# A two-layer diffusion trunk on one core: the first down projection turns finished rows into columns from the next group's fourth step on, and the first feed-forward's block sums are issued in three calls per channel group

## The chip, the core and the metric

The kernel runs on one core of a Trainium2 chip. The metric is the device time of one execution in microseconds (us); a few executions are timed and their median is given. Beside the timed runs one execution is profiled; every duration below comes from that one. The engines are TensorE (PE; its weight loads are listed as PEld), VectorE (DVE), ScalarE (ACT), GpSimd (POOL) and SyncE (SP), which only issues transfers. Each engine works through its own list of instructions in order, and waits at an instruction until what it needs is there. PEclk is the TensorE clock that was granted, as a share of full speed.

## The reference

Two layers over 1024 latent tokens and 256 context tokens, width 1024. Cut to what matters here:

```python
for l in range(2):
    h = rmsnorm(x, norm_mix_pre[l]) * (1 + sc1) + sh1      # latent and context apart
    m = hybrid_mixer(h, ...)      # attention heads and a conv + state-space scan, one in- and one out-projection
    x = x + g1 * rmsnorm(m, norm_mix_post[l])
    f = rmsnorm(x, norm_ffn_pre[l]) * (1 + sc2) + sh2
    y = (silu(f @ w_gate[l]) * (f @ w_up[l])) @ w_down[l]  # 1024 -> 2816 -> 1024
    x = x + g2 * rmsnorm(y, norm_ffn_post[l])
return x_lat                                               # context is not updated in the last layer
```

All of it is float32.

## The kernel before

**Products.** Each float32 product is made of three: weights and activations are split into a high part (a cast, on ACT, L114 for weights) and a low part (the difference, on POOL or DVE, L115), and `mm3` issues high*high, high*low and low*high on L228, L229 and L230. A weight tile is thus loaded raw (`raw_t`, `raw_u`; L126, issued by SP), cast by ACT, and subtracted by POOL; only then can PE use it (`w_t`, a ring of five).

**Rows and columns.** The residual stream x is kept as ten tiles of 128 tokens: tiles 0 and 1 are context, 2 to 9 latent. A projection needs it the other way round, with channels on the partitions. That takes a rescale of the rows by 1/rms (`pre_scale`: squares on ACT L243, the small sums and the root on POOL L245, L235 and L236, and the multiplication of the rows in place on POOL L375) and then a "flip": transposes on PE (L402 in `flip_steps`, two tiles and two channel blocks in one PSUM bank), two ACT evictions that apply scale and shift (L405), a high part on POOL (L409) and a low part on DVE (L410). The results are `hc` (context), `ha` and `hb` (the two halves of the latent tokens).

**The first feed-forward.** In layer 0, `ctx_gateup` multiplies the context by the gate and up weights, 22 steps of 128 hidden channels with 48 products of 256 columns each (0.118 us apiece). After each step it calls `next(fill)` once. The fill, `fill_c`, prepares the latent tokens for the gate and up projections that come next. These use seven block products in the place of eight, and so need sums and differences of 2x2 blocks: `quads` loads two flipped blocks (L1009), transposes two more (L1016, evicted by ACT on L1020), keeps one of them in DRAM (L1032, L1033), forms four differences on DVE and puts each with its high (ACT, L1025) and low part (L1026) into the blocks `T1` to `T4`. It does that for two pairs of tiles (i) and two channel groups (k2) each, and comes back to its caller once per channel group. In layer 1 the same `quads` is run to its end in one go.

**The down projection and its end.** `down_all` works in groups of tiles: in layer 0 tiles 0 to 3, then 4 to 6, then 7 to 9 (groups 0, 1 and 2 below). A group runs over 22 steps `ff`; a step multiplies one weight tile of 128x1024 with the hidden values of each tile of the group (`hid_ring`, loaded on L1201 by SP, eight slots in all), 6 products of 512 columns per tile. A tile's sums stay in two PSUM banks for the whole group; there are five banks of the kind `ps_w` and three of the kind `ps_s`. At the last step of a group `finish_psum` ends each tile: squares on ACT from the banks, the root on POOL, a multiplication on DVE (L832) that frees the banks, the addition to x (L838, on POOL for even tiles, on DVE for odd ones), and a store of the new x to DRAM, issued by ACT (L839). Then `done` hands the tile on: with every second tile it rescales the pair at once (`pre_scale`, in place, so it has to wait until the store has read the rows), and puts the pair's flip into the list `todo`. `flip` takes one step (four transposes and what follows) from that list after each step `ff` of groups 1 and 2:

```python
                    def done(t, y):
                        ys[t] = y
                        if t in pairs:
                            xs = [ys[t - 1], y]
                            k.pre_scale(xs)
                            todo.append(k.flip_steps(xs, *pairs[t], 1, 0))
```

What is left in the list (the last two pairs, which make `hb`) is flipped in layer 1, inside `xbc`, which starts layer 1's in-projection with a few products on `hc` and `ha`, goes on with those on `hb`, and copies each result into a row buffer on ACT (L483). Its conv weights are loaded on L463 and L464 and transposed on L466.

**What sets the order.** The code names the work in the order above, but a scheduler with its own estimates of durations and priorities decides in which order each engine's list is written. Moving a call in the code moves the instructions of every engine near it, and not always by as much as the code says.

Of the kernel before, what the change touches and what calls it, by code (L numbers as in the profile page):

```python
# [54 lines left out]
class Trunk:  # L55
# [945 lines left out]
    def quads(self, l, xs, i, B):  # L1001
        nc = self.nc
        cc = self.cols[l, 1]
        tt = nc.vector.tensor_tensor
        v = lambda a: a.rearrange("p (k n) -> p k n", k=2)
        for k2 in range(0, 4, 2):
            qa, qb = self.x(), self.x()
            for half in range(2):
                nc.sync.dma_start(qa[:, half * 512:(half + 1) * 512], self.hf_d[l][(k2 + 4 * half) // 2, i])  # L1009
            for half in range(2):  # L1010
                t = self.psw()
                for k in range(2):
                    kt = k2 + 4 * half + k
                    for j, a in enumerate(xs):
                        rows = a[half][:, kt % 4 * P:(kt % 4 + 1) * P] if isinstance(a, list) else a[:, kt * P:(kt + 1) * P]
                        nc.tensor.transpose(t[:, k * 256 + j * P:k * 256 + (j + 1) * P], rows, self.ident)  # L1016
                for k in range(2):
                    kt = k2 + 4 * half + k
                    o = half * 512 + k * 256
                    nc.scalar.activation(qb[:, o:o + 256], t[:, k * 256:(k + 1) * 256], AF.Identity, bias=cc[:, kt:kt + 1], scale=cc[:, 16 + kt:17 + kt])  # L1020
            b11, b21, b12, b22 = qa[:, 0:512], qa[:, 512:1024], qb[:, 0:512], qb[:, 512:1024]

            def put(name, src, eng):
                d = B[name][:, k2:k2 + 2, :, 256 * i:256 * i + 256]
                nc.scalar.copy(d[:, :, 0], v(src))  # L1025
                eng.tensor_tensor(d[:, :, 1], v(src), d[:, :, 0].bitcast(F32), op=ALU.subtract)  # L1026

            if l:
                put("B22", b22, nc.vector)
            else:  # L1030
                keep = self.s2()
                nc.gpsimd.tensor_scalar(keep, b22, 1.0, 1.0, op0=ALU.mult, op1=ALU.mult)  # L1032
                nc.scalar.dma_start(self.b22_d[k2 // 2, i], keep)  # L1033
            tt(b11, b12, b11, op=ALU.subtract)
            tt(b12, b22, b12, op=ALU.subtract)
            tt(b22, b22, b11, op=ALU.subtract)
            put("T2", b22, nc.vector)
            put("T3", b12, nc.vector)
            put("T1", b11, nc.vector)
            tt(b21, b22, b21, op=ALU.subtract)  # L1040
            put("T4", b21, nc.gpsimd)
            yield
# [163 lines left out]
    def down_all(self, l, hx, load, fill=lambda: None, done=lambda t, x: None):  # L1206
        loads = self.loads
        ahead = 9 if l else 8
        for n in range(3, ahead):
            load(n)  # L1210
        for n, (g, ff) in enumerate(loads):
            ts = self.GROUPS[l][g]
            if ff == 0:
                banks = [[a(), b()] for a, b in ((self.psw, self.psw), (self.psw, self.psw), (self.pss, self.pss), (self.psw, self.pss))[:len(ts)]]
            h, u = hx.pop(n), self.U[l, "d", g, ff]
            for i, t in enumerate(ts):
                for c in range(2):
                    s = slice(c * 512, (c + 1) * 512)
                    self.mm3(banks[i][c], (h[:, 0, i * P:(i + 1) * P], h[:, 1, i * P:(i + 1) * P]), (u[:, 0, 0, s], u[:, 1, 0, s]),
                             ff == 0, ff == NFF - 1)  # L1220
                if ff == NFF - 1:
                    done(t, self.finish_psum(l, t, banks[i]))
            self.free(l, "d", g, ff)
            load(n + ahead)
            if g:
                fill()

    def finish_psum(self, l, t, halves):
# [7 lines left out]
def emit(nc, tc, I, out, dump=None):  # L1236
    with ExitStack() as es:
        k = Trunk(nc, tc, es, I, out)
# [13 lines left out]
        def drain(*gs):  # L1252
            for g in gs:
                for _ in g:
                    pass

        for l in range(DEPTH):
# [62 lines left out]
            with tc.tile_pool(name=f"acc{l}", bufs=1, reuse_waits="tile") as accp:  # L1320
                if l == 0:
                    B = {}

                    def fill_c():
                        fl[2]()
                        yield
                        xs = [k.row_halves(t, 0) for t in (6, 7)]
                        B.update(k.blocks(accp))
                        yield
                        for i in range(2):  # L1330
                            k.pre_scale(xs)
                            yield
                            for _ in k.quads(0, xs, i, B):
                                yield
                            if i == 0:
                                xs = [k.row_halves(t, 0) for t in (8, 9)]
                                yield

                    k.spare = (lambda: accp.tile([P, 1024], F32, tag="raw", name="raw_u"),
                               lambda: k.grp.tile([P, 1024], F32, tag="grow", name="raw_u"))  # L1340
                    fc = fill_c()
                    k.ctx_gateup(0, fc)
                    drain(fc)
                    k.back22(B)

                    def fill_s():
                        yield from k.mod_stream(0, (5,), k.psw, True)
                        yield from k.mod_stream(1, (0, 1), k.psw, True)
                        cols = k.mod_cols(1, 0)
                        yield from k.mod_stream(1, (2,), k.psw, True)  # L1350
                        cols()
                        yield from k.mod_stream(1, (3, 4, 5), k.psw, True)

                    fs = fill_s()
                    hx, load = k.ffn(0, B, step(fs), accp)
                    drain(fs)
                    k.frow = [k.gate_row(0, 5, "norm_ffn_post", 0), k.gate_row(0, 5, "norm_ffn_post", 1, k.x())]
                    ys, todo = {}, []
                    pairs = {1: (SC, 0), 3: (SA, 0), 5: (SA, 1), 7: (SB, 0), 9: (SB, 1)}

                    def done(t, y):
                        ys[t] = y
                        if t in pairs:
                            xs = [ys[t - 1], y]
                            k.pre_scale(xs)
                            todo.append(k.flip_steps(xs, *pairs[t], 1, 0))

                    def flip():
                        while todo and next(todo[0], todo) is todo:
                            todo.pop(0)  # L1370

                    k.down_all(0, hx, load, flip, done)
                    late = [lambda: drain(todo.pop(0))] * len(todo)
                else:
                    B = k.blocks(accp)
                    B["B22"] = k.block22()
                    k.down_all(1, *k.ffn(1, B, lambda: None, accp, fl[2], [k.last_x[t] for t in (8, 9)]))
# [23 lines left out]
```

## Time and profile before

| | |
|---|---|
| median of 3 runs | 3217.45 us (3215.97 to 3223.33) |
| profiled execution, its own time | 3221.04 us |
| its span in the trace | 3219.3 us |
| mean granted TensorE clock | 0.973 |
| busy: PE, PEld | 94%, 78% |
| busy: DVE, ACT, POOL | 52%, 44%, 52% |

The profiled execution's own time is 1.7 us longer than its span and 3.6 us longer than the median. A row of the wait view reads: engine, the tile written and its line, "<-", the releaser with its tile and line, then the summed wait in us, the number of waits and the longest. A row of the timeline reads: start in us from the span's start, duration, engine, line, operation, out<-in, shapes, how many instructions were put together, and in brackets how long the engine had waited and for what. A row of the table by stretch reads: the stretch, its length, then the busy time (and number of instructions) of PE, PEld, DVE, ACT and POOL, the granted clock, the share of the DMA engines and GB/s.

### The profile page before, as it was taken

The page shows a single profiled execution, that of the slowest core. Times are in us where ns is not written, and L with a number is a line of the kernel's source. Part 1 is how long each engine was busy: PE and PEld are TensorE (multiplying, and loading weights), DVE is VectorE, ACT ScalarE, POOL GpSimd, SP SyncE. Part 2 cuts the span into 40 slices and gives each one's busy share as a digit, 9 for nine tenths or more (in the row PEclk, how much of TensorE's full clock was granted, in tenths as well). Part 3 has the DMA queues.
Part 4 walks back from the last instruction along what each step waited for, and adds up shares of the span by engine and source line. Part 5 has one row for each costly group of instructions (what it writes and reads, how often), then busy time and mean ns, then how long its engine had stood idle before and what let it go on. Part 6 is the DMA issues. An engine that isn't in the chain of part 4 may idle for free.

```text
span 3219.3 us, 45016 instructions
## 1 busy us (share of the span) xinstructions
PE 3034.8 (94%) x16147; PEld 2511.3 (78%) x16147; DVE 1679.0 (52%) x3093; ACT 1410.2 (44%) x2595; POOL 1668.3 (52%) x1529
## 2 busy tenths in 40 slices
PE   6899898999889999999998998899999899999997
PEld 4677687888789777778876777688888688888885
DVE  2556557666575555543021166768665766554003
ACT  4433336666664333332243344337666633333232
POOL 4326556544565444444476634755444555554663
PEclk8899899999999999999998999999999899999999
DMA  6276554222576545547566525653222443336776
GB/s 230 70 218 211 191 164 128 79 66 66 167 226 214 182 149 177 177 151 248 176 234 219 155 61 159 224 177 100 66 66 85 132 133 116 112 112 208 238 247 208
DMA packets 372703, 510.66 MB, mean 159 GB/s; under 512 B 25400, under 2 KB 258520, under 8 KB 372224
## 3 DMA queue, kind: packets, MB, share of 16 engines
q1 hardware_dynamic: 292912, 385.09, 38.4%
q10 hardware_dynamic: 79568, 122.69, 10.4%
q8 instruction: 128, 2.10, 0.3%
q14 instruction: 95, 0.78, 0.1%
HBM read 384.71 MB, written 122.99 MB: 158 GB/s over the span
## 4 chain that ended last, share of the span: by engine, by line
PE 51%; DMA 6%; POOL 4%; DVE 4%; ACT 2%; issue 2%; ACTq 0%; SPq 0%; DVEq 0%; POOLq 0%
PE ps_w L228 9%; PE ps_w L229 9%; PE ps_w L230 9%; PE ps_s L228 5%; PE ps_s L229 5%; PE ps_s L230 5%; DMA raw_t<-in_w_down 3%; POOL w_t L115 2%; PE ps_w L916 2%; PE ps_w L909 2%; PE ps_s L887 2%; ACT w_t L114 1%; PE ps_w L279 1%; DMA raw_t<-in_w_up 0%; PE ps_w L759 0%
## 5 line engine op out<-in xcount | busy, mean ns | idle before, releaser
L115 POOL TENSOR_TENSOR w_t<-raw_t,w_t 128x512 fp32r<-128x512 f32 (+2 forms) x430 | 797.4, 1865 | 812.2 <-ACT w_t L114 766.1
L114 ACT CAST w_t<-raw_t 128x512 fp32r<-128x512 f32 (+2 forms) x470 | 368.2, 799 | 715.2 <-PE ps_s L230 249.0
L888 DVE TENSOR_SCALAR_CACHE_REDUCE att_a<-ps_s 128x512 f32<-128x512 f32 (+1 forms) x400 | 227.0, 586 | 137.2 <-PE ps_s L887 128.3
L896 POOL TENSOR_SCALAR att_a<-att_a,att_st 128x1280 f32<-128x1280 f32 (+1 forms) x144 | 183.1, 1274 | 152.0 <-DVE att_st L895 82.7
L229 PE MATMUL ps_w<-w_t,hid_ring 128*128 128x512 f32 x523 | 207.1, 396 | 8.7 <-POOL w_t L115 8.7
L230 PE MATMUL ps_w<-w_t,hid_ring 128*128 128x512 f32 x523 | 205.7, 394 | 0.0
L894 ACT ACTIVATE att_a<-att_a,att_st 128x1280 f32<-128x1280 f32 (+1 forms) x144 | 183.2, 1273 | 34.5 <-DVE att_st L893 30.3
L909 PE MATMUL ps_w<-cst_all,att_a 128*128 128x128 f32 x1312 | 197.6, 276 | 0.1
L228 PE MATMUL ps_w<-w_t,hid_ring 128*128 128x512 f32 x523 | 195.6, 395 | 2.0 <-ACT w_t L114 1.4
L115 DVE TENSOR_TENSOR xt<-s2t,xt 128x512 fp32r<-128x512 f32 (+2 forms) x145 | 141.2, 975 | 57.7 <-ACT xt L114 55.5
L489 DVE SCALAR_TENSOR_TENSOR xt<-row,convw,xt 128x512 f32<-128x512 f32 (+1 forms) x128 | 125.3, 1032 | 83.9 <-ACT xt L487 64.4
L909 PEld LDWEIGHTS ps_w<-cst_all,att_a 128*128 128x128 f32 x1312 | 153.2, 141 | 11.3 <-DVE xt L832 5.5
L832 DVE SCALAR_TENSOR_TENSOR xt<-ps_w,rstd_t,gate_row 128x512 f32<-128x512 f32 x57 | 40.0, 745 | 232.3 <-POOL rstd_t L236 169.4
L114 ACT CAST xt<-s2t 128x512 fp32r<-128x512 f32 (+2 forms) x145 | 78.7, 543 | 152.5 <-DVE s2t L1145 63.3
L228 PE MATMUL ps_w<-ha,w_t 128*128 128x512 f32 x352 | 138.4, 394 | 2.3 <-ACT xt L1020 2.3
L229 PE MATMUL ps_w<-ha,w_t 128*128 128x512 f32 x352 | 138.5, 393 | 1.9 <-DVE ha L410 1.9
L230 PE MATMUL ps_w<-ha,w_t 128*128 128x512 f32 x352 | 138.0, 392 | 0.0
L229 PEld LDWEIGHTS ps_w<-w_t,hid_ring 128*128 128x128 f32 x523 | 98.7, 189 | 34.2 <-POOL w_t L115 12.1
L228 PEld LDWEIGHTS ps_w<-w_t,hid_ring 128*128 128x128 f32 x523 | 98.5, 189 | 25.3 <-ACT w_t L114 2.7
L115 DVE TENSOR_TENSOR w_t<-raw_t,w_t 128x1024 fp32r<-128x1024 f32 (+1 forms) x40 | 44.2, 1116 | 141.2 <-ACT w_t L114 141.2
L887 PE MATMUL ps_s<-att_c,raw_q 128*128 128x512 f32 (+1 forms) x400 | 109.3, 372 | 7.2 <-DMA raw_q<-q 6.8
L230 PEld LDWEIGHTS ps_w<-w_t,hid_ring 128*128 128x128 f32 x523 | 98.7, 189 | 21.5
(366 smaller groups left out, 8797.7 us busy)
## 6 DMA issues: line engine op xcount, KB each, us to landing
raw_t<-in_w_down SPq DMA_DIRECT2D x132, 512.0 KB
hid<-xt ACTq DMA_DIRECT2D x88, 512.0 KB
raw_t<-in_w_gate SPq DMA_DIRECT2D x70, 512.0 KB
hid_ring<-hid SPq DMA_DIRECT2D x85, 384.0 KB
xt<-in_w_mod SPq DMA_DIRECT2D x56, 512.0 KB
raw_t<-in_w_up SPq DMA_DIRECT2D x46, 512.0 KB
xt<-xs SPq DMA_DIRECT2D x36, 512.0 KB
raw_t<-in_w_in SPq DMA_DIRECT2D x32, 512.0 KB
```

Source lines behind the costliest of these rows:

```text
L114: self.nc.scalar.copy(hi, src)
L115: (eng or self.nc.vector).tensor_tensor(lo, src, hi.bitcast(F32), op=ALU.subtract)
L228: mm(out, st[0], mv[0], start=first, stop=False)
L229: mm(out, st[0], mv[1], start=False, stop=False)
L230: mm(out, st[1], mv[0], start=False, stop=last)
L489: nc.vector.scalar_tensor_tensor(acc, row[:, o0 + k:o0 + k + n], cw[:, ct, k:k + 1], acc, op0=ALU.mult, op1=ALU.add)
L887: nc.tensor.matmul(s[:, :m], qs[t][c][:, hd], kst[:, g, j:j + m], start=c == 0, stop=c == 1)
L888: nc.vector.tensor_scalar(pb[:, j:j + m], s[:, :m], -0.125, None, op0=ALU.mult, op1=ALU.min, accum_out=st[:, n:n + 1])
L894: nc.scalar.activation(pb, pb, AF.Exp, bias=nmx, scale=-1.0, accum_out=st[:, 4:5])
L896: nc.gpsimd.tensor_scalar(pb, pb, st[:, 5:6], 1.0, op0=ALU.mult, op1=ALU.mult)
L909: nc.tensor.transpose(tp[:, (2 * k + h) * P:(2 * k + h + 1) * P], pr[h][:, (k2 + k) * P:(k2 + k + 1) * P], self.ident)
L916: nc.tensor.matmul(av, vst[:, kt, g], pt[:, c, k * 256:(k + 1) * 256], start=kt == 0 and c == 0, stop=kt == nk - 1 and c == 1)
```

## The change

Three edits. In `quads` two more `yield`s cut each channel group into three calls: loads, transposes, evictions and the kept block; then three differences with their puts; then the last difference with its put. In `down_all` the call of the flip is left out after step 0 of a group. In `emit` the rescale of a pair is no longer done at the moment when the pair is finished, but by the first call of a generator `ready`, which then lets a call pass and flips from the third call after it on.

```diff
@@ quads
                 nc.scalar.dma_start(self.b22_d[k2 // 2, i], keep)
+            yield
             tt(b11, b12, b11, op=ALU.subtract)
...
             put("T1", b11, nc.vector)
+            yield
             tt(b21, b22, b21, op=ALU.subtract)
             put("T4", b21, nc.gpsimd)
             yield
@@ down_all
             load(n + ahead)
-            if g:
+            if g and ff:
                 fill()
@@ emit
+                    def ready(xs, span, i):
+                        k.pre_scale(xs)
+                        yield
+                        yield
+                        yield from k.flip_steps(xs, span, i, 1, 0)
+
                     def done(t, y):
                         ys[t] = y
                         if t in pairs:
-                            xs = [ys[t - 1], y]
-                            k.pre_scale(xs)
-                            todo.append(k.flip_steps(xs, *pairs[t], 1, 0))
+                            todo.append(ready([ys[t - 1], y], *pairs[t]))
```

No transfer and no arithmetic is added or taken away, and outside of three places every engine's list has the same rows in the same order. The three places follow.

**The context gate and up steps, ACT's list.** L114 with `raw_t` or `raw_u` is the cast of a weight tile, L114 with `s2t` and L1079 (L1077 before) belong to the step's own result, L1020 is the eviction of the transposes and L1025 the put of a block. Before, at the second pair of tiles:

```order
776 L114 CAST w_t<-raw_t 128x1024
777 L114 CAST xt<-s2t 128x256
778 L1081 DMA hid_120<-xt 256x1x256
779 L114 CAST w_t<-raw_u 128x1024
780 L114 CAST w_t<-raw_t 128x1024
781 L1020 ACTIVATE xt<-ps_w,cols_8075 128x256 x4
782 L1025 CAST h_hb<-xt 128x2x256
783 L1077 ACTIVATE s2t<-ps_w 128x256
784 L1025 CAST h_t_8637<-xt 128x2x256
785 L1033 DMA b_119<-s2t 128x512
786 L114 CAST xt<-s2t 128x256
787 L1020 ACTIVATE xt<-ps_w,cols_8075 128x256 x4
```

Now, at the same pair:

```order
796 L114 CAST w_t<-raw_t 128x1024
797 L114 CAST xt<-s2t 128x256
798 L1020 ACTIVATE xt<-ps_w,cols_8075 128x256
799 L1083 DMA hid_120<-xt 256x1x256
800 L1020 ACTIVATE xt<-ps_w,cols_8075 128x256 x3
801 L114 CAST w_t<-raw_u 128x1024
802 L1079 ACTIVATE s2t<-ps_w 128x256
803 L1025 CAST h_hb<-xt 128x2x256
```

The two channel groups of a pair, whose evictions stood six rows apart, are now about twenty rows apart (the next L1020 is row 820), and the casts of two weight tiles no longer stand directly ahead of the first eviction. On PE the transposes of the second pair (2 and 14 of them, at rows 3020 and 3069) become 2, 3 and 3 at rows 3212 to 3230 and 8 at row 3359; the 8 of the first pair's second channel group move from row 2875 to row 2971.

**The down projection, from group 1 to group 2, PE's list.** `ps_s_15183` is a bank of tile 9, `ps_w_15179` one of tile 7, `xt_15101` the new x of tile 4, and the five `w_t` of group 2's first steps are 15011, 15035, 15059, 15083 and 15165. Before, PE does the five steps of one bank of tile 9 (15 products), then one transpose of tile 4, and then the rest of group 2's first products:

```order
L229 MATMUL ps_s_15183<-w_t_15165,hid_ring_13732 128x512
L230 MATMUL ps_s_15183<-w_t_15165,hid_ring_13732 128x512
L402 MATMUL ps_w_15169<-cst_all_84,xt_15101 128x128
L228 MATMUL ps_w_15179<-w_t_15011,hid_ring_13732 128x512
L229 MATMUL ps_w_15179<-w_t_15011,hid_ring_13732 128x512
```

Now the first transpose of tile 4 stands 81 products after the start of group 2, and the other three of its flip step four products further on:

```order
L229 MATMUL ps_w_15172<-w_t_15149,hid_ring_13732 128x512
L230 MATMUL ps_w_15172<-w_t_15149,hid_ring_13732 128x512
L402 MATMUL ps_w_15247<-cst_all_84,xt_15121 128x128
L402 MATMUL ps_w_15247<-cst_all_84,xt_15101 128x128
L402 MATMUL ps_w_15247<-cst_all_84,xt_15121 128x128
L229 MATMUL ps_s_15173<-w_t_15149,hid_ring_13732 128x512
```

Group 2 now starts with a bank of tile 7 and one of tile 9 in turn (26 products), where before it was tile 9's bank alone.

**The same place, POOL's list.** L115 is the low part of a weight tile, L838 the addition to x, L375 the rescale of a tile's rows, L409 a part of a flip. Before:

```order
577 L115 TENSOR_TENSOR w_t<-raw_t,w_t 128x1024
578 L838 TENSOR_TENSOR xt<-xt 128x1024
579 L245 TENSOR_TENSOR ss_t<-ss_t 128x1
580 L235 TENSOR_SCALAR rstd_t<-ss_t 128x1
581 L236 TENSOR_TENSOR rstd_t<-rstd_t,mhalf 128x1
582 L375 TENSOR_SCALAR xt<-xt,rstd_t 128x1024
...
588 L375 TENSOR_SCALAR xt<-xt,rstd_t 128x1024
589 L236 TENSOR_TENSOR rstd_t<-rstd_t,mhalf 128x1
590 L838 TENSOR_TENSOR xt<-xt 128x1024
591 L409 TENSOR_SCALAR ha<-s2t 128x2x256
592 L115 TENSOR_TENSOR w_t<-raw_t,w_t 128x1024 x2
```

Now:

```order
577 L115 TENSOR_TENSOR w_t<-raw_t,w_t 128x1024
578 L245 TENSOR_TENSOR ss_t<-ss_t 128x1
579 L838 TENSOR_TENSOR xt<-xt 128x1024
...
582 L838 TENSOR_TENSOR xt<-xt 128x1024
583 L245 TENSOR_TENSOR ss_t<-ss_t 128x1 x2
584 L235 TENSOR_SCALAR rstd_t<-ss_t 128x1 x2
585 L236 TENSOR_TENSOR rstd_t<-rstd_t,mhalf 128x1 x2
586 L375 TENSOR_SCALAR xt<-xt,rstd_t 128x1024 x2
587 L115 TENSOR_TENSOR w_t<-raw_t,w_t 128x1024 x2
588 L409 TENSOR_SCALAR ha<-s2t 128x2x256
```

The rescales now stand together behind both additions, and still ahead of the next two weight parts (L115). On SP, the loads of four hidden slots now stand together ahead of the second weight load of group 2 after the loads of x (before, each had its turn with a weight).

**The end of layer 0's down projection, PE's list.** The last flips write the columns of `hb`. Before, four transposes stood among the products on `hc` and `ha` at row 6955, and the other 28 here:

```order
7099 L229 MATMUL ps_s<-ha,w_t 128x512
7100 L230 MATMUL ps_s<-ha,w_t 128x512
7101 L402 MATMUL ps_w<-cst_all,xt 128x128 x28
7102 L228 MATMUL ps_s<-hb,w_t 128x512 x3
7103 L229 MATMUL ps_s<-hb,w_t 128x512
```

Now all 32 stand here:

```order
7124 L229 MATMUL ps_s<-ha,w_t 128x512
7125 L230 MATMUL ps_s<-ha,w_t 128x512
7126 L402 MATMUL ps_w<-cst_all,xt 128x128 x32
7127 L228 MATMUL ps_s<-hb,w_t 128x512 x3
7128 L229 MATMUL ps_s<-hb,w_t 128x512
```

Between the last product of the down projection and this block there are as many products as before; only the four transposes at row 6955 are gone from among them. At the boundary from group 0 to group 1 the first some fifty products stand in the same order as before; the first flip comes 80 products after the group's start where it came after 76.

## The prediction

> **What bounds the kernel.** I read the page first, then the waits of PE in the stretches that the change touches, then their timelines, and last the table by stretch for PE's pace.
>
> ```profile
> span 3219.3 us, 45016 instructions
> PE 3034.8 (94%) x16147; PEld 2511.3 (78%) x16147; DVE 1679.0 (52%) x3093; ACT 1410.2 (44%) x2595; POOL 1668.3 (52%) x1529
> PE 51%; DMA 6%; POOL 4%; DVE 4%; ACT 2%; issue 2%; ACTq 0%; SPq 0%; DVEq 0%; POOLq 0%
> ```
>
> PE is busy for 94% of the span, no other engine for more than 52%, and PE has the largest share of the chain that ended last. No edit takes away a product. So the change can only pay through the 3219.3 - 3034.8 = 184.5 us in which PE stands still, and through a lower granted clock after such stops. The waits of PE in 870:950, inside the context's gate and up steps:
>
> ```profile
> PE ps_w L402 <- POOL xt L375: 6.1, 1, 6.1
> PE ps_w L1016 <- POOL s2t L375: 4.7, 3, 4.1
> PE ps_w L1016 <- ACT xt L1020: 4.3, 1, 4.3
> ```
>
> and in 1600:1870, from the end of group 0 to the first products on `hb`:
>
> ```profile
> PE ps_w L402 <- POOL xt L375: 12.9, 2, 9.2
> PE ps_s L229 <- POOL w_t L115: 3.9, 2, 2.9
> PE ps_s L228 <- POOL hb L409: 2.0, 1, 2.0
> PE ps_w L228 <- ACT w_t L114: 1.1, 1, 1.1
> PE ps_w L229 <- POOL w_t L115: 0.8, 1, 0.8
> PE ps_w L228 <- DVE xt L832: 0.6, 1, 0.6
> ...
> PE ps_s L228 <- ACT w_t L114: 0.5, 1, 0.5
> PE ps_s L228 <- ACT row L483: 0.5, 1, 0.5
> ```
>
> The largest are transposes (L1016, L402) that wait for rescaled rows (L375); the first list's 6.1 lies ahead of what the edits move. The timeline of PE places the others, in order the block sums, the end of group 0, the end of group 1 and the end of group 2:
>
> ```profile
> 927.29 0.33 PE L1016 MATMUL ps_w<-cst_all,s2t 128*128 128x128 f32 x1 [4.10 <-POOL s2t L375]
> 941.34 0.66 PE L1016 MATMUL ps_w<-cst_all,s2t 128*128 128x128 f32 x4 [4.26 <-ACT xt L1020]
> 1642.45 1.21 PE L228 MATMUL ps_w<-w_t,hid_ring 128*128 128x512 f32 x4 [1.07 <-ACT w_t L114]
> 1644.92 0.50 PE L229 MATMUL ps_w<-w_t,hid_ring 128*128 128x512 f32 x1 [0.79 <-POOL w_t L115]
> 1711.70 0.50 PE L229 MATMUL ps_s<-w_t,hid_ring 128*128 128x512 f32 x1 [1.06 <-POOL w_t L115]
> 1712.93 0.49 PE L228 MATMUL ps_s<-w_t,hid_ring 128*128 128x512 f32 x1 [0.50 <-ACT w_t L114]
> 1716.28 0.79 PE L229 MATMUL ps_s<-w_t,hid_ring 128*128 128x512 f32 x1 [2.85 <-POOL w_t L115]
> 1726.66 0.48 PE L402 MATMUL ps_w<-cst_all,xt 128*128 128x128 f32 x1 [9.16 <-POOL xt L375]
> 1832.14 0.55 PE L402 MATMUL ps_w<-cst_all,xt 128*128 128x128 f32 x3 [3.77 <-POOL xt L375]
> ```
>
> Then PE's pace, from the table by stretch (the stretch, its length, PE's busy time and products; after POOL's, the granted clock):
>
> ```profile
> 906.00:923.00 17.00, 17.00 (x144) 16.98 (x142) 16.55 (x18) 12.45 (x24) 8.48 (x5) 1.00 0.81 260
> 928.00:935.40 7.40, 7.40 (x50) 7.40 (x50) 5.28 (x4) 2.62 (x5) 7.13 (x6) 0.77 0.70 212
> 942.30:950.30 8.00, 8.00 (x55) 8.00 (x56) 7.22 (x11) 6.49 (x13) 2.82 (x4) 0.81 0.73 235
> 1726.70:1733.90 7.20, 7.20 (x25) 5.71 (x26) 1.41 (x2) 0.00 (x0) 5.18 (x8) 0.74 0.00 1
> 1735.00:1819.00 84.00, 84.00 (x368) 67.75 (x367) 2.77 (x4) 27.91 (x36) 53.24 (x26) 1.00 0.62 195
> 1832.40:1836.90 4.50, 4.50 (x27) 4.50 (x26) 3.56 (x5) 1.02 (x2) 4.23 (x7) 0.62 0.00 0
> 1842.80:1845.70 2.90, 2.90 (x26) 2.90 (x25) 1.80 (x2) 0.78 (x3) 2.63 (x4) 1.00 0.00 0
> ```
>
> Undisturbed, a product of 256 columns takes 17.00 / 144 = 0.118 us and one of 512 columns 84.00 / 368 = 0.228 us. Behind each of the long waits the clock is granted at 0.62 to 0.81, and the same products take longer.
>
> **The block sums (two more yields).** To be gained: 4.10 + 4.26 = 8.36 us of waits, and behind them 7.40 - 50 x 0.118 = 1.50 and 8.00 - 55 x 0.118 = 1.51; together 11.4. For the first wait, counted in the lists: the second pair's first rescale stood behind 65 weight parts of POOL and its first transposes behind 24 weights on PE; now it is 69 and 32. The distance grows by four weights of 24 products each, 4 x 24 x 0.118 = 11.3 us, which is more than the 4.10. For the second, the wait was for an eviction that stood behind two weight casts on ACT; now the cast ahead of it is that of the step's own result. What could be late next is the bank of the one remaining burst of eight transposes and the weights' arrival. Bounds: 0 and 11.4. I leave 1.4 for such remainders, a third of one of the two waits, and take 10.0. The loads of the blocks (L1009) and of the rows (L380) move later on SP past weight loads; as many transfers as before, and 906:923 shows PE without a stop at a DMA share of 0.81, so I cost that at nothing; the cover would be gone if that share were full. The differences on DVE are the same in number, hidden by an engine that is half idle.
>
> **Group 0 to group 1 (the rescale and the flip later).** To be gained: 1.07 + 0.79 = 1.86 us, both waits for a weight that POOL or ACT gave late while they rescaled. With the rescale a step later I take 1.8 (bounds 0 and, with the 0.6 for a bank, 2.5).
>
> **Group 1 to group 2.** To be gained: 1.06 + 0.50 + 2.85 + 9.16 = 13.57 us, and behind them 7.20 - 25 x 0.228 = 1.50; together 15.1. What is ready when:
>
> ```profile
> 1708.14 0.40 PE L228 MATMUL ps_s<-w_t,hid_ring 128*128 128x512 f32 x1
> ...
> 1718.58 1.82 ACTq L839 DMA_DIRECT2D xs<-xt  x2
> ...
> 1725.49 1.12 POOL L375 TENSOR_SCALAR xt<-xt,rstd_t 128x1024 f32<-128x1024 f32 x1 [2.39 <-DMA xs<-xt]
> 1728.20 1.12 POOL L375 TENSOR_SCALAR xt<-xt,rstd_t 128x1024 f32<-128x1024 f32 x1
> ...
> 1731.36 2.40 POOL L838 TENSOR_TENSOR xt<-xt 128x1024 f32<-128x1024 f32 x1 [1.52 <-DVE xt L832]
> 1736.45 2.68 POOL L115 TENSOR_TENSOR w_t<-raw_t,w_t 128x1024 fp32r<-128x1024 f32 x1 [0.31 <-ACT w_t L114]
> ```
>
> Group 2 begins at 1708.14. Its first flip comes after 81 products, 81 x 0.228 = 18.5, at 1726.6, and the other three transposes four products later, at 1727.6. The rows cannot be rescaled before the store has read them, 1725.49; two rescales in a row then end at 1725.49 + 2 x 1.12 = 1727.73. That leaves 0.1 to 1.1 of the 9.16; I take 1.0. Of the weights: the three short waits came because PE went through five weights within 15 products of one bank. Now it does 26 on two banks, which spreads the demand. The next weight part was at 1736.45 because the addition at 1731.36 and a flip stood ahead of it; now both additions are ahead of the rescales and it follows them: 1727.73 + 2.68 = 1730.4. PE has used up five weights after 5 x 18 = 90 products and a flip, 1708.14 + 90 x 0.228 + 0.5 + the 1.0 = 1730.2. I put 0.5 on that. So the addition is what decides: it was so late because tile 6's root stood behind a rescale that waited for the store; now it stands ahead of it. 15.1 - 1.0 - 0.5 = 13.6. Bounds: 15.1 above; below, a third rival.
>
> **The end of group 2.** To be gained: 3.77 of waiting, and 4.50 - 27 x 2.90 / 26 = 1.49 behind it, since the first four of the last 32 transposes no longer stand among the products on `hc` and `ha`. To be paid: they now stand in the block ahead of the first `hb` product, which the evictions pace.
>
> ```profile
> 1859.48 3.33 PE L402 MATMUL ps_w<-cst_all,xt 128*128 128x128 f32 x28
> 1864.78 0.96 PE L228 MATMUL ps_s<-hb,w_t 128*128 128x512 f32 x3 [1.97 <-POOL hb L409]
> ...
> 1860.16 6.50 ACT L405 ACTIVATE s2t<-ps_w,cols 128x256 f32<-128x256 f32 x14
> ...
> 1866.90:1870.40 3.50, 3.50 (x10) 2.71 (x9) 2.02 (x3) 0.00 (x0) 0.89 (x1) 0.51 0.00 0
> ```
>
> One flip step more is two evictions, 2 x 6.50 / 14 = 0.93 us later. And the products on `hc` now meet their banks sooner: I put one wait of each kind that the list above has for a bank at such a place, 0.6 (L832) and 0.5 (L483). 3.77 + 1.49 - 0.93 - 1.1 = 3.2. Bounds: 5.26 - 0.93 = 4.3 above, and -2.0 if the rows' wait only moves into the block.
>
> Here a rule stands against the change. The row: 28 transposes and a wait of 1.97, and behind them ten products in 3.50 us at a clock of 0.51, though PE stood still for only 1.97. The Trainium skill, "TensorE: Matmul & The Clock Gate", has in Part 1 that the clock falls to half after an idle window of about 3.4 us, and in Part 4 that transposes do not count as busy in the same way; the trace agrees, since 3.33 + 1.97 = 5.30 us is longer than such a window and 1.97 is not. By that rule 32 transposes and a wait longer by 0.93 make some 6.7 us, close to two windows, and a second one at half clock would cost half of 3.4, an estimate of 1.7 us: the sum would then be 1.7 lower. By the row alone the same half-clock stretch follows as before, and I go by that.
>
> **The sum.** 10.0 + 1.8 + 13.6 + 3.2 = 28.6 us. Against the profiled execution's own 3221.04 that is 3192.4. That execution is 3.6 us above the median of 3217.45; on the median's scale I forecast 3188.8. With every upper bound (11.4 + 2.5 + 15.1 + 4.3 = 33.3) it is 3184. A measurement of this kernel can tell about 0.2%, 6.4 us, from no change.
>
> **Rivals.** *The block sums keep their waits.* PE still meets the transposes in order; if the rows or the evictions come later by as much as the transposes were moved, the 10.0 stay: 3199. For it: the squares and loads of the second pair move later too, by some 19 rows of ACT's list. Against it: the count of weights above, which takes that into account.
>
> *The wait at group 1 to 2 takes another place.* If tile 6's addition still ends at 1731.36 + 2.40 = 1733.8, the two rescales ahead of which it now stands end 1733.8 + 1.5 (two roots) + 2.24 = 1737.5, and PE, there at 1726.6, waits 10.9 where the sum has 1.0, with 1.5 of half clock behind it: 11.4 are lost, and the time is 3200. For it: POOL works in order, and the addition waits for DVE. Against it: its root, the cause, is now ahead of the store's wait. Both rivals together give 3210.
>
> *The change moves the waits and no more.* Every pair still has to be rescaled and flipped; if each wait only turns up at the new place, the time stays within 0.2%, near 3217. Against it: in all three places there are products between the old place and the new.
>
> *Slower: weights starved in group 2.* Four loads of hidden values, which wait for slots that PE frees in steps 0 to 3, stand together ahead of a weight load on SP. If weights then stay late for the whole group, every step loses something. It would have to eat the 28.6 and 6.4 more, 35 us, in 22 steps: it decides from 1.6 us a step. Against it: 1735:1819 shows PE at 84.00 of 84.00 at a DMA share of 0.62, with cast and difference of a weight (2.68) well within a step of 18 x 0.228 = 4.1, so a late start is made good.
>
> **Chances.** The forecast (3181 to 3195, its own range) 0.62; block sums' waits stay 0.11; the wait at group 1 to 2 takes another place 0.13; both 0.05; waits only move 0.05; slower 0.04 (some 3224 or more). The first four are faster by over 0.2% (0.91, of which I move 0.01 to the middle, for more than one of them at once): faster 0.90, within 0.2% 0.06, slower 0.04. The range runs from 3181, the sum of upper bounds and 3 us of the runs' own scatter, to 3208, which leaves out the last two and part of "both".
>
> **What the profile after would show.** Right: no wait over 1.5 us at L1016 in the context steps and a clock of 1.00 there; behind group 1 a wait at L402 of about 1 us, and none over 1 for a weight; at the end of group 2 no L402 among the products on `hc` and `ha`, and 32 in the block, with a wait for `hb` of some 2 to 3 us. Wrong: an L402 wait for L375 near 10 us in group 2, a weight wait of several us in its sixth step, or L1016 waiting 4 us at its new place. A wait elsewhere, where the lists are the same, would show that a queue's timing, not its order, has shifted.

## Result and the profile after

| | before | after |
|---|---|---|
| median of 10 runs | 3218.14 us (3201.55 to 3223.85) | 3199.07 us (3184.87 to 3206.26) |
| ratio, 95% interval | | 0.9945 [0.9928, 0.9962] |
| profiled execution, its own time (span) | 3221.04 us (3219.3) | 3196.39 us (3194.6) |

The ratio is a gain of 17.7 us (12.2 to 23.2). The forecast was a gain of 28.6 us; the gain is 0.62 of that. The time lies in the range of 3181 to 3208 us, but not in the part from 3181 to 3195 that was the forecast's own. The page of after:

```profile
span 3194.6 us, 45008 instructions
PE 3029.0 (95%) x16147; PEld 2508.9 (79%) x16147; DVE 1674.6 (52%) x3093; ACT 1410.6 (44%) x2595; POOL 1663.9 (52%) x1529
```

The two profiled executions differ by 24.65 us, more than the medians. 5.5 us of that lie ahead of the first place that the change touches, where every list has the same rows: PE begins the context steps at 861.64 before and at 856.11 after. This is scatter: in the ten profiles of the table the context steps begin between 844.48 (E1) and 861.64, though PE's rows ahead of them are the same in all. Behind the last stage of the table after takes 2.73 us longer than before, again with the same rows. So the comparison is made stage by stage, between PE's first products of each stage. E1 to E9 are the experiments below (there is no E3 and no E7):

| us, by stage | before | after | E1 | E2 | E4 | E5 | E6 | E6b | E8 | E9 |
|---|---|---|---|---|---|---|---|---|---|---|
| context gate and up (block sums) | 156.95 | 154.20 | 153.88 | 157.42 | 156.79 | 152.76 | 145.44 | 144.42 | 154.92 | 144.29 |
| latent gate and up | 484.69 | 488.58 | 487.96 | 485.08 | 484.84 | 489.53 | 490.92 | 489.69 | 489.11 | 487.19 |
| sum of these two | 641.64 | 642.78 | 641.84 | 642.50 | 641.63 | 642.29 | 636.36 | 634.11 | 644.03 | 631.48 |
| down projection | 315.74 | 296.99 | 313.13 | 297.00 | 297.09 | 297.00 | 297.09 | 297.00 | 303.33 | 297.42 |
| from there to the first `hb` product | 45.76 | 41.49 | 45.92 | 42.24 | 42.27 | 41.51 | 41.51 | 41.52 | 46.88 | 41.51 |

The down projection and its end gained 18.75 + 4.27 = 23.0 us. The two stages with the block sums lost 1.1. The same is seen in PE's waits. Of the down projection and its end (1590:1850), after:

```profile
PE ps_s L228 <- POOL hb L409: 2.1, 1, 2.1
PE ps_s L228 <- DVE xt L832: 0.7, 1, 0.7
PE ps_s L229 <- DVE hb L410: 0.6, 1, 0.6
PE ps_w L228 <- DVE xt L832: 0.6, 1, 0.6
PE ps_s L228 <- ACT row L483: 0.5, 1, 0.5
PE ps_w L402 <- ACT s2t L405: 0.3, 1, 0.3
```

No transpose waits for a rescale any more, where it was 12.9 us, and no product for a weight, where it was 6.3 in all. Of the context steps and the first latent products (870:1035), after:

```profile
PE ps_w L402 <- POOL xt L375: 6.1, 1, 6.1
PE ps_w L1016 <- POOL s2t L375: 4.6, 2, 2.4
PE ps_w L228 <- ACT s2t L1079: 4.4, 2, 2.6
PE ps_w L1016 <- ACT w_t L114: 1.4, 1, 1.4
PE ps_w L279 <- DMA xt<-in_w_mod: 0.9, 1, 0.9
PE ps_w L228 <- ACT s2t L405: 0.8, 1, 0.8
```

The first row is the wait that the edits don't touch, and the last one was there before too. The transposes L1016 wait for their rescaled rows as long as before (4.6 us now, 4.7 before); the 4.3 us for an eviction became 1.4 for a weight cast and 4.4 for banks (L1079 is ACT's eviction of a context product, L1077 before). Of these 4.4, 2.6 lie at the first latent products, and so do the 0.9 for a load (L279, a product that fills in there): most of what the latent stage lost.

### The profile page after: what moved, and what is told of

It reads as the page before. It is cut to its first block, busy times and chain, and to the rows that moved or that the text cites. A ratio compares the mean times of both kernels' runs of the same rounds, so it can differ in the third digit from the quotient of the medians.

```text
span 3194.6 us, 45008 instructions
## 1 busy us (share of the span) xinstructions
PE 3029.0 (95%) x16147; PEld 2508.9 (79%) x16147; DVE 1674.6 (52%) x3093; ACT 1410.6 (44%) x2595; POOL 1663.9 (52%) x1529
## 4 chain that ended last, share of the span: by engine, by line
PE 74%; DMA 8%; DVE 6%; POOL 5%; issue 3%; ACT 3%; SPq 0%; ACTq 0%; DVEq 0%; POOLq 0%
PE ps_w L228 12%; PE ps_w L230 12%; PE ps_w L229 12%; PE ps_s L228 7%; PE ps_s L229 7%; PE ps_s L230 7%; PE ps_w L916 5%; PE ps_w L909 4%; PE ps_s L887 4%; POOL w_t L115 3%; DMA raw_t<-in_w_down 2%; PE ps_w L279 1%; ACT w_t L114 1%; PE ps_w L765 1%; PE ps_w L759 1%
## 5 line engine op out<-in xcount | busy, mean ns | idle before, releaser
L115 POOL TENSOR_TENSOR w_t<-raw_t,w_t 128x512 fp32r<-128x512 f32 (+2 forms) x430 | 795.9, 1861 | 812.6 <-ACT w_t L114 760.9
L114 ACT CAST w_t<-raw_t 128x512 fp32r<-128x512 f32 (+2 forms) x470 | 368.3, 800 | 707.1 <-PE ps_s L230 240.3
L115 DVE TENSOR_TENSOR xt<-s2t,xt 128x512 fp32r<-128x512 f32 (+2 forms) x145 | 139.7, 964 | 57.1 <-ACT xt L114 55.5
L114 ACT CAST xt<-s2t 128x512 fp32r<-128x512 f32 (+2 forms) x145 | 78.7, 542 | 157.1 <-DVE s2t L1147 63.0
L115 DVE TENSOR_TENSOR w_t<-raw_t,w_t 128x1024 fp32r<-128x1024 f32 (+1 forms) x40 | 43.7, 1105 | 141.7 <-ACT w_t L114 141.7
```

What stands on the lines that cost most here:

```text
L114: self.nc.scalar.copy(hi, src)
L115: (eng or self.nc.vector).tensor_tensor(lo, src, hi.bitcast(F32), op=ALU.subtract)
```

## Experiments

All ratios are to the kernel before, with a 95% interval. The changed kernel's own is 0.9945 [0.9928, 0.9962].

**E1, the block sums alone, and E2, the flip edits alone.** Which edit brought the gain?

```diff
 E1 = before, with
+            yield        # in quads, after the kept block
+            yield        # in quads, after put("T1", ...)
 E2 = after, without these two
```

> The two yields in quads alone; the down projection as before. Theory A (the waits for the block sums came back at their new place and were partly handed on to the first gate/up products of the latent tokens, since SP issues the second pair's row loads behind later weight loads): the time is that of the kernel before within 0.1%, ratio 0.999 to 1.002, and the trace has waits of 4 to 5 us at L1016 for L375, one near 1.8 us for a bank in the context steps, and one near 2.6 us behind the first latent products. Theory B (the prediction's term: the waits go): 10 us less, ratio 0.997.

> The later rescale and the skipped first call alone; quads as before. Theory A: all of the change's gain, 19 to 23 us, ratio 0.993 to 0.994, with no wait at L402 between the groups; the waits of 4.1 and 4.3 us at L1016 are those of before. Theory B (both edits share the gain of 17.7 us measured for the whole): 8 to 10 us, ratio 0.997.

E1: 3220.51 us, 1.0025 [1.0006, 1.0043]. E2: 3196.20 us, 0.9944 [0.9924, 0.9964]. Theory A holds in the stages: in E2 the down projection takes 297.00 us, as in the changed kernel, and the two waits at L1016 are as before (4.5 and 4.7 us). The flip edits are the whole gain, and the block sums are worth nothing or cost a little. Both ratios lie a little above theory A's own numbers (0.999 to 1.002, 0.993 to 0.994). The waits of E1 in 875:1035:

```profile
PE ps_w L1016 <- POOL s2t L375: 4.5, 2, 2.3
PE ps_w L228 <- ACT s2t L1079: 4.0, 2, 2.2
PE ps_w L1016 <- ACT w_t L114: 1.4, 1, 1.4
PE ps_w L279 <- DMA xt<-in_w_mod: 0.6, 1, 0.6
```

They are those of after, or a little shorter. That E1 is slower by 2 to 14 us is more than its profiled execution shows, which was the fastest of its twelve (the two stages sum to 0.2 us more than before); this part is open.

**E4, the rescale inside the flip's generator, with the flip still called at step 0.**

```diff
 E4 = E2, with
-            if g and ff:
+            if g:
```

> Only the rescale inside the flip's generator (with its two passed calls); step 0 of a group calls the flip as before, and quads is as before. Theory A1 (moving the rescale is what orders POOL's list and puts the first transposes 81 products later; the skipped call adds nothing to it): within 2 us of the run with both flip edits, ratio 0.993 to 0.995. Theory A2 (the skipped call is needed, since a call at step 0 rescales one step earlier, still ahead of the weights): a wait of several us at L402 or for a weight in group 2 is left, ratio 0.996 to 0.998.

3195.17 us, 0.9945 [0.9925, 0.9966], and each stage within 0.7 us of E2's. Theory A1 holds: the skipped call adds nothing, and PE's transposes between the groups stand behind the same number of products in both traces. The moved rescale, with the two calls that it lets pass, is the edit that counts.

**E8, the rescale at once, the flip three calls later.** The moved rescale does two things: it orders POOL's list, and it puts the transposes later on PE. E8 undoes the first.

```diff
                     def ready(xs, span, i):
-                        k.pre_scale(xs)
+                        yield
                         yield
                         yield
...
                         if t in pairs:
-                            todo.append(ready([ys[t - 1], y], *pairs[t]))
+                            xs = [ys[t - 1], y]
+                            k.pre_scale(xs)
+                            todo.append(ready(xs, *pairs[t]))
```

> The changed kernel with the rescale back at the moment the pair is finished, but the flip three calls later: PE has its first transposes of group 2 after 67 products, POOL's list is as before the change (tile 6's addition behind two rescales that wait for the store). Theory P (POOL's order makes the wait): rows ready at 19 to 22 us after the last products of tiles 4 and 5 and the sixth weight as late as before; the down projection takes 6 to 12 us more than in the changed kernel (296.5 us there, 315.5 before). Theory Q (the transposes' place on PE makes it): it takes at most 4 us more.

3209.19 us, 0.9975 [0.9956, 0.9995]. The down projection takes 6.3 us more than in the changed kernel, at the lower edge of theory P's number, and P's mechanism is only partly there. The waits of PE from group 1 to group 2 (1700:1760) in E8:

```profile
PE ps_w L402 <- POOL xt L375: 1.5, 2, 1.0
PE ps_w L229 <- POOL w_t L115: 1.0, 2, 0.8
PE ps_s L228 <- DVE xt L832: 0.8, 1, 0.8
PE ps_w L228 <- ACT w_t L114: 0.4, 1, 0.4
```

Against 13.57 us before, 3.7 are left. So with the transposes later and POOL's list nearly as before, 12.4 of the 18.75 us come; the other 6.3 need POOL's order too. Neither theory was right alone. The split is rough: in E8 the first transpose of group 2 stands 67 products after the group's start where the changed kernel has 81, and POOL's order with the old place on PE was not run. The end of group 2 gained nothing here (46.88 us): with the rows rescaled at once, 12, 4 and 16 transposes stand at three places, and the longest wait of E8's list for 1600:1860 is one of 5.8 us at L402 among them.

**E5, the row loads of tiles 8 and 9 three calls earlier.** What makes the block sums wait at their new place? SP issues these loads behind weight loads, so they were the first suspect. By the edit they are asked for three calls earlier (the expectation counts two); on SP they then go out four weight loads earlier.

```diff
-                            for _ in k.quads(0, xs, i, B):
+                            for n, _ in enumerate(k.quads(0, xs, i, B)):
+                                if (i, n) == (0, 3):
+                                    late_xs = [k.row_halves(t, 0) for t in (8, 9)]
                                 yield
                             if i == 0:
-                                xs = [k.row_halves(t, 0) for t in (8, 9)]
+                                xs = late_xs
                                 yield
```

> The changed kernel, with the row loads of tiles 8 and 9 asked for two calls earlier (four places earlier on SP, ahead of four weight loads); the transposes keep their places on PE. Theory A (those loads are what the rescale and the transposes wait for): the waits at L1016 of 2.4, 1.4 and 2.2 us go, and what is left is the bank wait and the wait at the first latent products; 4 to 7 us less than the changed kernel, ratio to the kernel before 0.992. Theory C (ACT's and POOL's lists set those waits, whenever the rows land): no difference from the changed kernel beyond 2 us.

3196.59 us, 0.9956 [0.9935, 0.9977]; the sum of the two stages is 642.29, where after has 642.78. Theory A falls: the waits for L375 did go, but others took their place. Theory C has the time right, though not the waits. In 895:1012, E5:

```profile
PE ps_w L228 <- ACT s2t L1079: 3.9, 3, 1.9
PE ps_w L1016 <- ACT s2t L1079: 1.8, 1, 1.8
PE ps_w L230 <- POOL w_t L115: 1.3, 1, 1.3
PE ps_w L228 <- DVE s2t L1080: 1.2, 2, 0.9
```

Nearly all of these are for ACT, or for what follows ACT. So something earlier may hold ACT. Its timeline in the changed kernel shows a candidate, with the rows of SP and DVE that lead to it:

```profile
892.60 1.56 SPq L1009 DMA_DIRECT2D xt<-hf  x2
...
896.00 1.06 ACT L114 CAST w_t<-raw_u 128x1024 fp32r<-128x1024 f32 x1
...
899.38 0.69 DVE L1035 TENSOR_TENSOR xt<-xt 128x512 f32<-128x512 f32 x1 [5.79 <-DMA xt<-hf]
...
900.10 0.62 ACT L1025 CAST h_hb<-xt 128x512 fp32r<-128x512 f32 x1 [3.04 <-DVE xt L1035]
...
900.63 0.38 ACT L1079 ACTIVATE s2t<-ps_w 128x256 f32<-128x256 f32 x1
```

The block's loads are issued at 892.60, the first difference on DVE can begin at 899.38, and ACT, whose next row is the put of that difference, stands for 3.04 us. Behind it in ACT's list stand a bank eviction and the next weight casts. The same happens at each of the four channel groups. After, 870:985, the waits of DVE and ACT for this:

```profile
DVE xt L1035 <- DMA xt<-hf: 16.0, 4, 5.8
ACT h_hb L1025 <- DVE xt L1035: 6.8, 4, 3.0
```

Before, DVE met such a wait at one group only (5.53 us, and ACT then stood 2.79).

**E6, the block's loads one call ahead, and E6b, the rows ahead too.** The rows come three calls earlier, as in E5; the expectation counts one.

```diff
 E6 = after, with (in quads, between the loads and the transposes)
                 nc.sync.dma_start(qa[:, half * 512:(half + 1) * 512], self.hf_d[l][(k2 + 4 * half) // 2, i])
+            yield
 E6b = E5 with the same line, and (i, n) == (0, 5) in the place of (0, 3)
```

> The changed kernel, with the two loads of a block step (L1009) asked for one call before the transposes instead of in the same call. Theory D (ACT's list stands 3 us at the first put of each step, because the difference on DVE waits for these loads to land, and the weight casts and the bank evictions behind it on ACT come late; the row loads were only the next in the line): the waits for the put on ACT go, the waits of PE in the context steps fall from 7.8 to under 4 us, and from the first context product to the first product of the down projection it takes 5 to 8 us less than in the changed kernel (642.8 us there, 641.6 before the change). Theory S (the stage is bound by the supply of weights, so that whatever is saved comes back as another wait): that time stays at 641 to 643 us.

> The same with the row loads of tiles 8 and 9 one call earlier too. Theory D: 6 to 9 us less than the changed kernel from the first context product to the first one of the down projection, and no wait at the transposes for L375; ratio to the kernel before 0.991 to 0.993. Theory S: the same 641 to 643 us, ratio 0.994.

E6: 3187.03 us, 0.9910 [0.9886, 0.9934]; E6b: 3187.84 us, 0.9906 [0.9882, 0.9931]. Theory D's times hold: the sum of the two stages falls by 6.4 and 8.7 us against after, and in E6 only 0.8 us of waits are left in the context steps from 880 us on. DVE's waits for the block loads are gone in E6, E6b and E9. ACT's stand at the first put got shorter but did not go, as theory D had it; in E6, 870:985:

```profile
ACT h_hb L1026 <- DVE xt L1036: 3.9, 4, 1.7
```

The edit does a second thing: with one more call, the transposes also come a call later behind the rescale, and their wait for L375 falls from 4.6 to 0.4 us without earlier rows. E5 shows that nothing is gained when this wait alone goes; how much of the 6.4 us needs both was not run. In E6b the block sums cost PE next to no wait. All that the view shows for 880:1040 is

```profile
PE ps_w L228 <- ACT s2t L1080: 3.5, 1, 3.5
```

and in the table by stretch, 80 us of it read:

```profile
880.00:960.00 80.00, 80.00 (x671) 80.00 (x670) 59.02 (x59) 48.77 (x83) 50.57 (x33) 1.00 0.86 257
```

Theory S is right in one point: some comes back. In E6b the context steps are 9.8 us shorter than in after, the sum of the two stages only 8.7, and against before it is 12.5 and 7.5. The one wait left, 3.5 us, is at the second half of the first latent products.

**E9, the flip edits, and `quads` in two calls: loads, then all the rest.**

```diff
 E9 = E2, with (in quads, between the loads and the transposes)
+            yield
```

> The flip edits of the change, and quads in two calls per channel group: loads in the first, everything else in the second. Theory D: the waits of 4.1 and 4.3 us go with little in their place, 5 to 9 us less than the kernel with the flip edits alone, ratio to the kernel before 0.992. Theory S: 641 to 643 us from the first context product to the first of the down projection, ratio 0.994 as for the flip edits alone.

3189.74 us, 0.9915 [0.9890, 0.9940]. The sum of the two stages is 10.2 us below that of before and 11.0 below that of E2: this is the size of the 10.0 that the prediction had put on the block sums, had by one yield at another place. The waits in 890:1010, E9:

```profile
PE ps_w L228 <- DVE s2t L1079: 1.3, 1, 1.3
PE ps_w L228 <- ACT s2t L1078: 0.7, 1, 0.7
PE ps_w L1017 <- POOL s2t L375: 0.2, 1, 0.2
```

By their ratios to before, E6, E6b and E9 are 0.003 to 0.004 below the changed kernel (9.7 to 12.5 us), with intervals that overlap its own; it is the stage times that tell them from it. Among the three these runs make no difference.

**The wait at the first latent products.** It was read from the traces, not isolated by a run. After, in order of the chain:

```profile
1015.73 0.37 SPq L209 DMA_DIRECT2D raw_t<-in_w_gate  x1
...
1019.80 1.14 ACT L114 CAST w_t<-raw_t 128x512 fp32r<-128x512 f32 x2 [5.22 <-DMA raw_t<-in_w_gate]
1020.84 0.38 ACT L1079 ACTIVATE s2t<-ps_w 128x256 f32<-128x256 f32 x1
...
1021.27 0.50 PE L228 MATMUL ps_w<-h_t,w_t 128*128 128x512 f32 x1 [2.62 <-ACT s2t L1079]
```

The last context bank is evicted behind a weight cast that waits for its load. Before, that load went out 1.65 us after PE's first latent product, and PE did not wait; in E9 it was 3.84 and the wait 0.73, in after 5.42 and 2.62, in E6 6.34 and 3.57. The last of the block sums is ready 59.0 us ahead of the first latent product before, 37.1 in E9, 22.8 in after and 1.7 in E6. So in these four, the later the block sums end, the later that load goes out and the longer the wait; that the one makes the other is argued, not shown.

## Why the prediction was right or wrong

**Block sums: wrong.** 10.0 us were forecast; the context steps gained 2.75 and the latent ones lost 3.89. Of the signs named ahead, no wait over 1.5 us at L1016 and a clock of 1.00 did not come: the transposes waited 2.4 and 2.2 us for their rows, and the mean clock was 0.94 in 880:960. The rival "the block sums keep their waits", to which 0.11 was given, came true. That the median falls on its time (3199) is partly luck: by the stages the flip edits gave 4.4 us more than the 18.6 that the sum had for them, the block sums cost 1.1, and the rest is scatter.

Two steps failed. The first is the count of weights between rescale and transposes (four more, 11.3 us). It measured the distance on POOL and PE only, as if the rescale came as early as POOL's list allowed; but SP now issued the rows' loads behind seven more weights. The loads of tiles 8 and 9 and their last rescale, before:

```profile
913.54 1.97 SPq L380 DMA_DIRECT2D s2t<-xs  x4
...
935.11 1.36 POOL L375 TENSOR_SCALAR s2t<-s2t,rstd_t 128x512 f32<-128x512 f32 x2
```

and after:

```profile
932.97 1.96 SPq L380 DMA_DIRECT2D s2t<-xs  x4
...
949.13 2.33 POOL L375 TENSOR_SCALAR s2t<-s2t,rstd_t 128x512 f32<-128x512 f32 x2
```

Counted from PE's first context product, the loads went out 25.0 us later (51.9, now 76.9), the last rescale ended 20.5 us later and the first transposes of the pair came 22.2 us later: the distance hardly grew. The second is that the loads moved past weight loads on SP were costed "at nothing", with a DMA share of 0.81, a mean over 17 us, as the cover. From the issue of the first group's block loads to their use, after, the table by stretch has

```profile
892.60:899.40 6.80, 6.80 (x59) 6.73 (x59) 0.69 (x2) 3.16 (x6) 4.47 (x4) 1.00 0.96 295
```

so that the share was all but full just then, and the cover gone by the prediction's own condition. PE was still busy in these 6.8 us; ACT stood for 3.0 of them. Before, the first group met the same (0.96 in 899.60:906.40), the later ones did not wait for their loads; after, all four did. E5 repaired the first alone and gained nothing; E6 moved the block's loads ahead of their use and gained 6.4 us; E9 did it in two calls per channel group and had the full term. The worry about the bank and the weights' arrival, on which 1.4 was put, was right in kind: the bank of the last context product cost 2.62.

**Group 0 to 1 and 1 to 2: right, and too small.** 1.8 + 13.6 = 15.4 were forecast, 18.75 measured. Taken between the same products of the two traces, the first boundary gave 2.25 us (from the 530th product of the stage to the 840th) and the second 16.71 (from there to the 1020th), which is more than its upper bound of 15.1. All waits went, as the sum had it, and the rescale came earlier than it said. POOL after:

```profile
1705.72 2.39 POOL L838 TENSOR_TENSOR xt<-xt 128x1024 f32<-128x1024 f32 x1
...
1711.63 2.41 POOL L838 TENSOR_TENSOR xt<-xt 128x1024 f32<-128x1024 f32 x1 [1.52 <-DVE xt L832]
...
1716.22 2.24 POOL L375 TENSOR_SCALAR xt<-xt,rstd_t 128x1024 f32<-128x1024 f32 x2 [0.18 <-DMA xs<-xt]
1718.41 4.76 POOL L115 TENSOR_TENSOR w_t<-raw_t,w_t 128x1024 fp32r<-128x1024 f32 x2
```

The rescales waited 0.18 for the store where it had been 2.39, and ended at 1718.46, 17.0 us after group 2's first product where the sum had 19.6; PE's first transpose of group 2 ran at 1720.35 without a wait. So the 1.5 us left for a remainder were not needed. The other part is the clock. The table by stretch for the whole down projection, before

```profile
1503.30:1818.80 315.50, 299.46 (x1297) 240.34 (x1296) 29.71 (x29) 97.42 (x147) 192.31 (x127) 0.97 0.63 204
```

and after:

```profile
1498.90:1795.40 296.50, 295.91 (x1297) 239.03 (x1295) 30.09 (x29) 97.50 (x147) 193.39 (x127) 1.00 0.67 217
```

The same 1297 matmuls (products and transposes) were busy for 3.55 us less, at a mean clock of 1.00 where it was 0.97. The sum had put 1.50 on that, from the one stretch behind the longest wait; the shorter waits ahead of it were followed by slow products too (in 1709.50:1717.50 the clock was 0.74). The rival of a wait at another place did not come: tile 6's addition ended at 1714.0, well ahead of the rescales. In E8, with POOL's order as before, a third of the gain is lost (6.3 of 18.75); so this order, which the prediction called what decides, was not the larger part.

**The end of group 2: right.** 3.2 forecast, 4.27 measured. The block of transposes after:

```profile
1831.74 7.41 ACT L405 ACTIVATE s2t<-ps_w,cols 128x256 f32<-128x256 f32 x16
...
1837.37 0.96 PE L228 MATMUL ps_s<-hb,w_t 128*128 128x512 f32 x3 [2.07 <-POOL hb L409]
```

and, from the table by stretch, what stands behind it:

```profile
1838.70:1842.20 3.50, 3.27 (x8) 2.59 (x9) 2.81 (x4) 0.45 (x1) 1.67 (x2) 0.51 0.00 0
1843.00:1848.00 5.00, 5.00 (x23) 4.12 (x23) 0.00 (x0) 0.00 (x0) 0.00 (x0) 1.00 0.00 0
```

ACT's evictions took 7.41 - 6.50 = 0.91 us more (0.93 in the sum). Of the banks, 0.7 was new, where 1.1 was put; the 0.5 at L483 had been there before and was counted twice. The sum also left out that the four transposes' own time, some 0.5 us (4/28 of 3.33, an estimate), leaves their old place. The second slow stretch, for which the prediction weighed 1.7 us against this term, did not come: there is one stretch of 3.50 us at a mean clock of 0.51, as before, and the clock is 1.00 behind it.

**Slower, and waits that only move.** For the whole kernel neither came; for the block sums, the second is what happened. The weights of group 2 were not late: no wait for one is left in the list above.

## What to carry to other kernels

When work that fills in between is spread over more steps, ask for its loads a step ahead of their first use. Judge the cover by the DMA share between issue and use and not by the mean of a stage, and look in every in-order list for what then stands behind the first instruction that needs them: here a list that stopped for 3 us had the next weights and banks behind it. When one wait of PE went (E5), waits for those came instead. A wait for one thing that goes away tells little; compare the time of the whole stage and of the next one. Where a finished tile is rescaled in place, put the rescale behind the other work that its queue owes the matmuls, and its reader as far on as the new group's products reach.

## What was not expected of the hardware

A load of two blocks (L1009) had its first user start 6.8 us after issue. The mean DMA share of that stage is 0.74, but 0.96 in those 6.8 us, behind two weight loads of 512 KB each that SP had issued in the 1.5 us ahead: a mean over a stage hides such a stretch. A share that high did not hold PE up by itself. In E6b, with the loads asked for ahead, PE kept its pace for 80 us at a mean share of 0.86 and 257 GB/s (880:960: 80.00 of 80.00 us busy, clock 1.00), with 0.99 in 884:892.
